# Other chunk sizes, a new order of the blocks, and one more block in paired products, in a two-layer trunk kernel

## The chip, the core and the metric

The kernel runs on one core of one Trainium2 chip. The metric is device time in microseconds, the median of three executions. Before the change these are 264.13, 264.52 and 264.88 us.

## What is computed

Two layers, each with three groups of attention heads side by side, on 256 tokens of width 1024, all in fp32. Cut to what matters here:

```python
h = rms_norm(x, norm_g[layer])
sb_q, sb_k, sb_v, sb_g, mb_q, mb_k, mb_v, mb_g, mem_q, mem_g = split(h @ w_in[layer])   # 8 x 384 and 2 x 256 columns
o_sb  = stick_breaking_attention(sb_q, sb_k, sb_v) * silu(sb_g)          # 6 heads of 64
o_mb  = softmax_attention(rotary(mb_q), rotary(mb_k), mb_v) * silu(mb_g) # 6 heads, causal
mk, mv = split(rms_norm(mem, mem_norm_g[layer]) @ w_mem_kv[layer])       # 256 memory tokens, 2 x 256 columns
o_mem = memory_attention(mem_q, mk, mv) * silu(mem_g)                    # 4 heads
x = x + concat(o_sb, o_mb, o_mem) @ w_out[layer]
```

With 256 tokens and blocks of 256 keys, the block-sparse attention `mb` has one block only and is plain causal attention. A last RMSNorm follows the second layer.

## The kernel before, in words

**Products.** Every projection is a "piece": `sb_qk` (768 columns, first of layer 0), the others with 384 or 256 columns, and `wo0` and `wo1` (512 columns each of `w_out`). Each has 8 blocks of 128 rows, k = 0 to 7. The product runs in fp32r. A weight w is split into hi (w rounded to fp32r) and lo (w - hi), the activations likewise, and three products are added: hi x hi, hi x lo, lo x hi. The split weights go to the buffer `hl`, HLC = 6144 weight columns wide (a column here is one column of one k block, 128 values). The activations' hi and lo halves stand side by side in `T`.

**Paired products.** A piece whose name stands in `DBL` (lines 85 and 86) takes two of its three products in one. `tr_k` (line 593, weights stationary, tokens moving) then issues, for each 128 columns and each k, one product of 512 columns (hi weights against the hi and lo activations) and one of 256 (lo weights against hi). A piece outside `DBL` takes three of 256. The two halves of the paired result are added when the bank is emptied. For a gate, `gate_evac` (line 940) does that with a copy on ACT and an addition on DVE, and in layer 0 a further multiplication by the row scale `rbx` on DVE. Without the pair it is one multiplication on DVE where `rbx` is there.

**Weights.** A piece is loaded in chunks of `NK` or `NKP` k blocks (lines 28 to 31). A chunk is one DMA from SP's queue into `raw`. ACT then rounds it into hi (`hi_task`, line 504; `DVE_HI` is added to DVE's price so that ACT gets all but two), and DVE subtracts (`lo_task`, line 513). TensorE may use a chunk when its hi and its lo are whole. `load_task` (line 522) lets at most `LOADS` chunks be under way: chunk j waits until chunk j - LOADS has landed.

**The order.** Every engine's instruction stream is written out by a planner, `Sched` (lines 117 to 237). Each part of the work is a task with a priority, a smaller number going first. The planner picks the step that can start earliest by its own estimates, and among those that start within a slack (`SLACK`, `SLACK_PE`) the one of smallest priority. On the chip the engines follow that order and wait for each other by semaphores. `PRI` and the constants `P_...` are priorities. `urgent` (line 529) gives the splitting of weights the priority -5 as long as it is at most `URG` chunks ahead of the chunk that TensorE is at, and 60 beyond that. The pieces' order in a layer is `ORDER`. A piece in `KMAJ` runs k outside and its parts inside, the others the parts outside. The `x` transposed slices and other inputs are loaded behind given chunks (`X_AT`, `X0_AT`, `X1_AT`, `CST_AT`). `xT` slice k is needed for k block k of `sb_qk`.

**Attention.** Scores (`pair_scores`, line 782) use 64 rows of the array, values (`pair_task`, line 901) 64 columns, both for a pair of heads. So TensorE changes its tile shape when it goes there and back; one such stay is called a visit here. `SCG` and `PVG` say which pairs are ready to run together as a group, `CROWD` and `HOLD` how many others, or how long, a lone pair waits for company. Between the two, softmax or stick-breaking runs on ACT and DVE, and the weights are transposed through DRAM (`trip`, line 1018; trips in `HALVES` come back in eight DMAs, the others in four). `DVE_W` shifts the choice of the engine that normalises softmax weights. A pair's values are multiplied with the silu of its gate (`ev`), split into `mxhi` and `mxlo`, and then the pieces `wo0` and `wo1` run, k = 0 to 3 of both first in layer 0. `silu_task` (line 965) takes the gates named together in `SILU`: it loads the silu table into ACT, runs, and loads the table of exp and ln back.

**Between the layers**, the last products of `wo1` give the residual, its row statistics and norm, and sixteen transposes on TensorE give the next layer's `T`. The first piece of layer 1 is a memory piece, which needs none of that.

Of the kernel before, what the change touches and what calls it, by code (L numbers as in the profile page):

```python
# [25 lines left out]
HLC = 6144  # L26
RAWC = 17664 - 2 * HLC
NK = {256: 3, 384: 2, 512: 2, 768: 1}
NKP = {("sb_k", 0): 4, ("sb_v", 0): 4, ("sb_v", 1): 4, ("sb_g", 1): 1, ("mb_q", 1): 3, ("mb_k", 1): 1, ("mb_v",
       1): 3, ("mb_g", 0): 4, ("mb_g", 1): 4, ("mem_q", 0): 1, ("mem_q", 1): 4, ("mem_g", 0): 2, ("mem_g",  # L30
       1): 2, ("mk", 0): 4, ("mv", 1): 2, ("wo0", 0): 1, ("wo0", 1): 1, ("wo1", 0): 1, ("wo1", 1): 1}
KSPLIT = (4, 4)
KMAJ = (("sb_q", 1), ("sb_g", 0), ("mb_q", 1), ("mb_k", 0), ("mb_k", 1), ("mb_v", 0), ("mb_g", 1), ("mem_g",
        0), ("mem_g", 1), ("mk", 1), ("mv", 0), ("mv", 1))
NTRIP = (0, 0)
KORD = ((0, 1, 2, 3, 4, 5, 6, 7), (6, 7, 4, 5, 2, 3, 0, 1))
LAT_SAME, LAT_CROSS = 130.0, 240.0
# [1 line left out]
NORM_LATE = 1029.7  # L39
DG_LATE = 885.3  # L40
COLD = 3900.0
PRI = ({"sb": (-1630, -1778), "mb": (-1356, -1226), "mem": (-2596, -720)}, {"sb": (-1368, -1432), "mb": (-1664,
       -2820), "mem": (388, 534)})
P_EV = -1323
P_H0 = 1640
P_RX = -1156
P_M0 = -1936
P_RM = 417
P_M1 = 86
URG = 4  # L50
X_AT = {4: 4, 7: 5, 8: 6, 9: 7}
CST_AT = 18
X0_AT = 9
X1_AT = 10
DMA_GBS = {"w1": 340.0, "w15": 350.0, "w3": 410.0, "dump": 250.0, "ret": 257.0}
RING = 8
SP_ISSUE = 450.0
# [4 lines left out]
TRIP_LAT = 500.0  # L62
ML_W = 0.0
ML_T = 200.0
ML_S = 800.0
SPLIT = (30,)
LOADS = 9
P_LD = -31914
MEM_AT = 0
ORDER = (["sb_qk", "mb_k", "mb_q", "mv", "mem_q", "sb_v", "mb_v", "mk", "sb_g", "mb_g", "mem_g"], ["mk",  # L70
         "mb_k", "mb_q", "mv", "mem_q", "mem_g", "sb_k", "sb_q", "sb_v", "mb_v", "mb_g", "sb_g"])
NCH = {"sb": 3, "mb": 3, "mem": 2}
SILU = ((("sb", "mb"), ("mem",)), (("sb",), ("mb", "mem")))
TABLE = 1290.0
P_SILU = -372
SCG = (((("sb", 2), ("sb", 1)), (("sb", 0), ("mb", 1), ("mb", 0)), (("mb", 2),), (("mem", 1),), (("mem", 0),)),
       ((("sb", 1), ("sb", 2), ("mb", 0)), (("mem", 0), ("mb", 1)), (("mem", 1), ("mb", 2)), (("sb", 0),)))
PVG = (((("mem", 0), ("mb", 2)), (("sb", 2), ("mb", 1), ("mb", 0)), (("sb", 1),), (("mem", 1),), (("sb", 0),)),
       ((("mb", 1), ("sb", 0), ("mb", 2), ("mem", 1)), (("sb", 2), ("sb", 1)), (("mem", 0),), (("mb", 0),)))
HOLD = 15360.0  # L80
HALVES = [("F", 1, "sb", 2), ("F", 1, "mb", 0)]
CROWD = 190
SPARE1 = 2
SPARE2 = 2
DBL = (("sb_qk", 0), ("sb_q", 1), ("sb_k", 1), ("sb_g", 1), ("mb_g", 0), ("mb_g", 1), ("mem_q", 0), ("mem_q",
       1), ("mem_g", 0), ("mem_g", 1), ("mk", 0), ("mk", 1), ("mv", 1))
DVE_W = -295.9
AHEAD = 106
DVE_HI = 42039.2
SLACK_PE = 170.0  # L90
SLACK = 20.0


def _free(ap):
# [145 lines left out]
def hybrid_trunk(ctx: ExitStack, tc: tile.TileContext, x, mem, norm_g, w_in, w_mem_kv, w_out,  # L240
# [150 lines left out]
    class Piece:  # L391
        def __init__(self, name, layer, src, width):
            self.name, self.layer, self.width, self.src = name, layer, width, src
            self.nk = NKP.get((name, layer), NK[width])
            self.kord = KORD[layer] if name[:2] == "wo" else tuple(range(KT))
# [238 lines left out]
    def piece_steps(p, n):  # L634

        if (p.name, p.layer) in KMAJ:
            return [(k, c) for k in range(KT) for c in range(n)]
# [511 lines left out]
    def main():  # L1149
# [25 lines left out]
        for l in range(DEPTH):  # L1175
# [15 lines left out]
            def T_piece(n, X, nchunk, need, post):  # L1191
                p = pieces[n, l]
                accs = {}
                for k, c in piece_steps(p, nchunk):
# [6 lines left out]
                    if k == KT - 1:  # L1201
                        S.spawn(post(c, accs[c]), P_EV, S.cur.t)

# [20 lines left out]
            for h in range(SBH):  # L1224
                S.spawn(scan_head(l, h), PRI[l]["sb"][1] + h)
            for h in range(MEMH):
                S.spawn(soft_head(l, h, "mem"), PRI[l]["mem"][1] + h)
            for h in range(SBH):
# [159 lines left out]
```

## Time and profile before

| | |
|---|---|
| median of three executions | 264.52 us |
| the profiled execution | 263.76 us |
| its span, first to last instruction | 262.0 us |
| TensorE busy | 255.6 us, 98%, 1573 products |
| its weight loads | 226.2 us, 86% |
| DVE busy | 223.5 us, 85%, 530 instructions |
| ACT busy | 193.8 us, 74%, 420 instructions |
| moved by DMA | 67.05 MB, 256 GB/s over the span |
| granted TensorE clock | 0.996 of full speed |

The profile lists each engine's busy time, the groups of instructions by line with their mean duration, the waits with who ended them, and the chain of work that ended last. A product's time from the start of one to the start of the next is shorter than its listed duration, since products overlap. So the text works with stretches of the trace that hold a counted number of products. PE is TensorE, PEld its weight loads, and `L299` line 299 of the kernel, where all DVE operations on two tensors are issued, whatever they work on; the names of the tiles tell them apart.

### The profile page before, as it was taken

How to read it: one execution, taken by the hardware profiler on the slowest of the kernel's cores; microseconds unless marked ns; L12 is line 12 of the kernel's file. 1: busy time of each engine (PE TensorE's matmuls, PEld its weight loads, DVE VectorE, ACT ScalarE, POOL GpSimd, SP SyncE). 2: the span in 40 equal slices, each digit the busy share in tenths (PEclk: the TensorE clock that was granted, in tenths of full speed). 3: DMA queues.
4: the chain of work that ended last, by engine and by line, in shares of the span. 5: the costliest groups of instructions: out<-in, count | busy, mean ns of one | idle time of the engine just before them, and what ended most of it. 6: DMA issues, size and time to landing. Idle time of an engine off the chain costs nothing.

```text
span 262.0 us, 4829 instructions
## 1 busy us (share of the span) xinstructions
PE 255.6 (98%) x1573; PEld 226.2 (86%) x1573; DVE 223.5 (85%) x530; ACT 193.8 (74%) x420; POOL 6.4 (2%) x18
## 2 busy tenths in 40 slices
PE   8999999999999999999999999999999999999991
PEld 5889999899899787878889998888899998788881
DVE  3876999999799999999899876779999999967454
ACT  3879996998797499994866654576958999786034
POOL 1001110001000000000000000000000000000000
PEclk9999999999999999999999999999999999999998
DMA  6999989999898999988665789784588888961004
GB/s 209 381 403 395 389 263 338 298 296 333 267 287 270 282 330 301 308 260 282 170 224 177 262 301 319 211 252 169 150 283 307 299 277 253 285 197 51 0 0 160
DMA packets 50200, 67.05 MB, mean 256 GB/s; under 512 B 4544, under 2 KB 41792, under 8 KB 50176
## 3 DMA queue, kind: packets, MB, share of 16 engines
q1 hardware_dynamic: 49232, 64.85, 77.4%
q0 software_dynamic: 512, 1.31, 1.7%
q10 hardware_dynamic: 432, 0.59, 0.7%
q8 instruction: 12, 0.20, 0.3%
q14 instruction: 12, 0.10, 0.1%
HBM read 57.29 MB, written 9.44 MB: 255 GB/s over the span
## 4 chain that ended last, share of the span: by engine, by line
PE 95%; ACT 1%; DMA 1%; DVE 0%; issue 0%; SPq 0%; DVEq 0%; ACTq 0%
PE bank L276 94%; DMA uT<-xT_dram 1%; PE bank L282 1%; ACT junk L295 1%; ACT ss L295 0%; DVE xs L299 0%; ACT T L295 0%; SPq L381 0%; DVE xs L307 0%; ACT xs L295 0%; DVEq L1384 0%; ACTq L295 0%
## 5 line engine op out<-in xcount | busy, mean ns | idle before, releaser
L299 DVE TENSOR_TENSOR hl<-raw,hl 128x512 fp32r<-128x512 f32 (+6 forms) x126 | 101.9, 825 | 7.8 <-ACT hl L293 5.7
L276 PE MATMUL bank<-T,hl 128*128 128x512 f32 (+1 forms) x606 | 104.5, 332 | 0.3 <-ACT T L295 0.3
L276 PEld LDWEIGHTS bank<-T,hl 128*128 128x128 f32 x606 | 90.2, 189 | 13.2 <-issue 1.2
L293 ACT CAST hl<-raw 128x512 fp32r<-128x512 f32 (+6 forms) x124 | 88.6, 740 | 16.9 <-PE bank L276 6.7
L276 PE MATMUL bank<-hl,T 128*128 128x384 f32 (+2 forms) x464 | 79.5, 330 | 0.0
L276 PEld LDWEIGHTS bank<-hl,T 128*128 128x128 f32 x464 | 77.5, 188 | 1.4 <-issue 0.7
L276 PE MATMUL bank<-hl,mxhi 128*128 128x512 f32 (+1 forms) x144 | 41.3, 367 | 0.0
L276 PEld LDWEIGHTS bank<-hl,mxhi 128*128 128x128 f32 x144 | 26.1, 189 | 5.0 <-ACT T L295 0.4
L276 PE MATMUL bank<-hl,mxlo 128*128 128x512 f32 (+1 forms) x72 | 26.4, 367 | 0.0
L295 ACT ACTIVATE junk<-xs 128x512 bf16<-128x512 f32 (+1 forms) x12 | 7.3, 611 | 17.6 <-DVE xs L299 16.2
L894 DVE STREAM_TRANSPOSE D<-w 128x384 f32<-128x384 f32 (+1 forms) x32 | 18.9, 594 | 0.4 <-ACT w L295 0.2
L295 ACT ACTIVATE w<-w,st 128x256 f32<-128x256 f32 (+1 forms) x32 | 14.1, 457 | 5.2 <-DVE st L847 4.5
L276 PEld LDWEIGHTS bank<-hl,mxlo 128*128 128x128 f32 x72 | 13.6, 188 | 2.2
L827 DVE TENSOR_TENSOR_SCAN a<-a,a 128x256 f32<-128x256 f32 (+1 forms) x24 | 12.7, 534 | 0.1
L295 ACT ACTIVATE T<-uT,gc 128x256 fp32r<-128x256 f32 x24 | 10.9, 508 | 2.0 <-DMA uT<-xT_dram 2.0
L303 DVE SCALAR_TENSOR_TENSOR T<-uT,gc,T 128x256 fp32r<-128x256 f32 x24 | 11.2, 480 | 0.9 <-ACT T L295 0.9
L295 ACT ACTIVATE a<-a 128x384 f32<-128x384 f32 x24 | 11.6, 522 | 0.2
L295 ACT ACTIVATE a<-bank 128x384 f32<-128x384 f32 x24 | 11.3, 483 | 0.0
L293 ACT COPY gT<-bank 128x256 f32<-128x256 f32 x13 | 4.8, 373 | 8.4 <-PE bank L276 8.2
L299 DVE TENSOR_TENSOR xs<-bank,xs 128x512 f32<-128x512 f32 (+1 forms) x8 | 5.2, 655 | 6.6 <-PE bank L276 6.6
L307 DVE TENSOR_SCALAR w<-w,st 128x256 f32<-128x256 f32 (+1 forms) x32 | 9.0, 324 | 0.1
L299 DVE TENSOR_TENSOR ev<-bank,gT 128x256 f32<-128x256 f32 x16 | 6.3, 417 | 1.5 <-ACT gT L295 1.4
(107 smaller groups left out, 217.9 us busy)
## 6 DMA issues: line engine op xcount, KB each, us to landing
raw<-in_w_in_dram SPq DMA_DIRECT2D x34, 384.0 KB, 6.0
raw<-in_w_out_dram SPq DMA_DIRECT2D x32, 256.0 KB, 5.0
Z<-D SPq DMA_DIRECT2D x16, 384.0 KB, 5.3
raw<-in_w_in_dram SPq DMA_DIRECT2D x7, 768.0 KB, 7.0
raw<-in_w_in_dram SPq DMA_DIRECT2D x18, 192.0 KB, 4.6
raw<-in_w_in_dram SPq DMA_DIRECT2D x4, 576.0 KB, 4.4
uT<-memT_dram SPq DMA_DIRECT2D x8, 256.0 KB, 6.8
raw<-in_w_in_dram SPq DMA_DIRECT2D x8, 256.0 KB, 5.5
```

The costliest lines, as they stand in the source:

```text
L276: nc.tensor.matmul(out, lhsT=lhsT, rhs=rhs, start=start, stop=stop, **kw)
L282: nc.tensor.transpose(out, in_, idt)
L293: nc.scalar.copy(out, in_)
L295: nc.scalar.activation(out, in_, func, **kw)
L299: nc.vector.tensor_tensor(out, a, b, op=op)
L303: nc.vector.scalar_tensor_tensor(out, a, s, b, op0=op0, op1=op1)
L307: nc.vector.tensor_scalar(out, a, s, None, op0=op)
L827: nc.vector.tensor_tensor_scan(a[:, r0:r1], a[:, r0:r1], u[:, r0:r1], 0.0, OP.add, OP.add)
L894: nc.vector.transpose(o, w[:, :n * 128].rearrange("p (m j r) -> p m j r", j=4, r=32))
```

## The change

Only constants change; no function does. With the chunk sizes given, the chunks are 138 in place of 126: 67 in place of 63 in layer 0, and 71 in place of 63 in layer 1. `("sb_g", 0)` joins `DBL`. The silu groups of layer 0 are three in place of two, the value groups there four in place of five. Ten loads may be under way in place of nine. `URG` goes from 4 to 63, and the slacks and all priorities get other values.

```diff
--- before.py
+++ after.py
@@ -26,12 +26,12 @@
 HLC = 6144
 RAWC = 17664 - 2 * HLC
 NK = {256: 3, 384: 2, 512: 2, 768: 1}
-NKP = {("sb_k", 0): 4, ("sb_v", 0): 4, ("sb_v", 1): 4, ("sb_g", 1): 1, ("mb_q", 1): 3, ("mb_k", 1): 1, ("mb_v",
-       1): 3, ("mb_g", 0): 4, ("mb_g", 1): 4, ("mem_q", 0): 1, ("mem_q", 1): 4, ("mem_g", 0): 2, ("mem_g",
-       1): 2, ("mk", 0): 4, ("mv", 1): 2, ("wo0", 0): 1, ("wo0", 1): 1, ("wo1", 0): 1, ("wo1", 1): 1}
+NKP = {("sb_k", 0): 4, ("sb_k", 1): 1, ("sb_v", 0): 1, ("sb_v", 1): 1, ("sb_g", 0): 4, ("mb_q", 0): 1, ("mb_q",
+       1): 1, ("mb_k", 1): 4, ("mb_v", 0): 1, ("mb_v", 1): 4, ("mb_g", 0): 3, ("mem_q", 0): 1, ("mem_g", 1): 1,
+       ("mk", 1): 1, ("mv", 0): 4, ("mv", 1): 2, ("wo0", 0): 3, ("wo0", 1): 3, ("wo1", 0): 3}
 KSPLIT = (4, 4)
-KMAJ = (("sb_q", 1), ("sb_g", 0), ("mb_q", 1), ("mb_k", 0), ("mb_k", 1), ("mb_v", 0), ("mb_g", 1), ("mem_g",
-        0), ("mem_g", 1), ("mk", 1), ("mv", 0), ("mv", 1))
+KMAJ = (("sb_q", 1), ("sb_v", 1), ("sb_g", 1), ("mb_q", 1), ("mb_v", 0), ("mb_g", 1), ("mem_q", 1), ("mem_g",
+        0), ("mem_g", 1), ("mv", 0))
 NTRIP = (0, 0)
 KORD = ((0, 1, 2, 3, 4, 5, 6, 7), (6, 7, 4, 5, 2, 3, 0, 1))
 LAT_SAME, LAT_CROSS = 130.0, 240.0
@@ -39,19 +39,19 @@
 NORM_LATE = 1029.7
 DG_LATE = 885.3
 COLD = 3900.0
-PRI = ({"sb": (-1630, -1778), "mb": (-1356, -1226), "mem": (-2596, -720)}, {"sb": (-1368, -1432), "mb": (-1664,
-       -2820), "mem": (388, 534)})
-P_EV = -1323
-P_H0 = 1640
-P_RX = -1156
-P_M0 = -1936
-P_RM = 417
-P_M1 = 86
-URG = 4
-X_AT = {4: 4, 7: 5, 8: 6, 9: 7}
-CST_AT = 18
+PRI = ({"sb": (-1812, -2078), "mb": (-1828, -1422), "mem": (-2720, -1120)}, {"sb": (-1568, -1708),
+       "mb": (-1916, -3416), "mem": (-810, 1014)})
+P_EV = -1461
+P_H0 = 1010
+P_RX = -1030
+P_M0 = -1630
+P_RM = 359
+P_M1 = -270
+URG = 63
+X_AT = {4: 4, 5: 5, 6: 6, 11: 7}
+CST_AT = 24
 X0_AT = 9
-X1_AT = 10
+X1_AT = 11
 DMA_GBS = {"w1": 340.0, "w15": 350.0, "w3": 410.0, "dump": 250.0, "ret": 257.0}
 RING = 8
 SP_ISSUE = 450.0
@@ -62,33 +62,33 @@
 TRIP_LAT = 500.0
 ML_W = 0.0
 ML_T = 200.0
-ML_S = 800.0
+ML_S = 300.0
 SPLIT = (30,)
-LOADS = 9
-P_LD = -31914
+LOADS = 10
+P_LD = -24288
 MEM_AT = 0
-ORDER = (["sb_qk", "mb_k", "mb_q", "mv", "mem_q", "sb_v", "mb_v", "mk", "sb_g", "mb_g", "mem_g"], ["mk",
-         "mb_k", "mb_q", "mv", "mem_q", "mem_g", "sb_k", "sb_q", "sb_v", "mb_v", "mb_g", "sb_g"])
+ORDER = (["sb_qk", "mb_q", "mb_k", "sb_v", "mem_q", "mk", "mv", "mb_g", "mb_v", "sb_g", "mem_g"], ["mv",
+         "mb_q", "mb_k", "mk", "mb_g", "mem_q", "sb_k", "sb_q", "mb_v", "sb_v", "mem_g", "sb_g"])
 NCH = {"sb": 3, "mb": 3, "mem": 2}
-SILU = ((("sb", "mb"), ("mem",)), (("sb",), ("mb", "mem")))
+SILU = ((("sb",), ("mb",), ("mem",)), (("sb",), ("mb", "mem")))
 TABLE = 1290.0
-P_SILU = -372
-SCG = (((("sb", 2), ("sb", 1)), (("sb", 0), ("mb", 1), ("mb", 0)), (("mb", 2),), (("mem", 1),), (("mem", 0),)),
-       ((("sb", 1), ("sb", 2), ("mb", 0)), (("mem", 0), ("mb", 1)), (("mem", 1), ("mb", 2)), (("sb", 0),)))
-PVG = (((("mem", 0), ("mb", 2)), (("sb", 2), ("mb", 1), ("mb", 0)), (("sb", 1),), (("mem", 1),), (("sb", 0),)),
-       ((("mb", 1), ("sb", 0), ("mb", 2), ("mem", 1)), (("sb", 2), ("sb", 1)), (("mem", 0),), (("mb", 0),)))
-HOLD = 15360.0
-HALVES = [("F", 1, "sb", 2), ("F", 1, "mb", 0)]
-CROWD = 190
+P_SILU = 934
+SCG = (((("sb", 2), ("sb", 0)), (("sb", 1), ("mb", 0), ("mb", 1)), (("mem", 1),), (("mem", 0),), (("mb", 2),)),
+       ((("mb", 0), ("sb", 0)), (("mb", 1), ("mem", 0), ("mb", 2)), (("sb", 1), ("sb", 2)), (("mem", 1),)))
+PVG = (((("mb", 0), ("sb", 2), ("sb", 1), ("mb", 1)), (("mem", 0), ("mb", 2)), (("mem", 1),), (("sb", 0),)),
+       ((("mem", 1), ("sb", 0), ("mb", 1), ("mem", 0)), (("mb", 2), ("sb", 1)), (("mb", 0),), (("sb", 2),)))
+HOLD = 12000.0
+HALVES = [("F", 1, "mb", 2)]
+CROWD = 104
 SPARE1 = 2
 SPARE2 = 2
-DBL = (("sb_qk", 0), ("sb_q", 1), ("sb_k", 1), ("sb_g", 1), ("mb_g", 0), ("mb_g", 1), ("mem_q", 0), ("mem_q",
-       1), ("mem_g", 0), ("mem_g", 1), ("mk", 0), ("mk", 1), ("mv", 1))
-DVE_W = -295.9
-AHEAD = 106
-DVE_HI = 42039.2
-SLACK_PE = 170.0
-SLACK = 20.0
+DBL = (("sb_qk", 0), ("sb_q", 1), ("sb_k", 1), ("sb_g", 0), ("sb_g", 1), ("mb_g", 0), ("mb_g", 1), ("mem_q",
+       0), ("mem_q", 1), ("mem_g", 0), ("mem_g", 1), ("mk", 0), ("mk", 1), ("mv", 1))
+DVE_W = 504.1
+AHEAD = 51
+DVE_HI = 63339.2
+SLACK_PE = 10.0
+SLACK = 0.0
 
 
 def _free(ap):
```

## The prediction

> **What bounds the kernel now.** First the page's busy times and its chain that ended last, then the waits of TensorE, then the chain in order of time.
>
> ```profile
> PE 255.6 (98%) x1573; PEld 226.2 (86%) x1573; DVE 223.5 (85%) x530; ACT 193.8 (74%) x420; POOL 6.4 (2%) x18
> ```
>
> ```profile
> PE 95%; ACT 1%; DMA 1%; DVE 0%; issue 0%; SPq 0%; DVEq 0%; ACTq 0%
> ```
>
> ```profile
> PE bank L276 <- PEq L1372: 0.8, 1, 0.8
> PE bank L276 <- ACT T L295: 0.3, 1, 0.3
> ```
>
> ```profile
> 4.59 128.15 PE bank L276 x796
> ...
> 139.26 114.49 PE bank L276 x696
> ...
> 258.25 0.33 DVEq L1384
> ```
>
> TensorE starts its real work at 4.59 us and is on the chain from there until 139.26 + 114.49 = 253.75 us, with only the sixteen transposes between the two long rows, which are TensorE's too. Its two waits, 1.1 us in all, lie in the first microseconds. So what the change can win lies in the 4.59 us before, in the last 262.0 - 253.75 = 8.25 us, in the number of products, and in what it costs to change tile shape. What it can lose is anything that comes later than TensorE wants it. DVE at 85% and ACT at 74% are not bounds over the whole span, but both are nearly full in stretches, so their order matters.
>
> A busy TensorE may still be slow inside, so I take counted stretches: the piece `sb_g` of layer 0 (72 products of 256 columns), a run of paired products in layer 1 (36 of 512 and 36 of 256; the count in the row holds a neighbour or two at the edges), and two visits for values, of 8 and of 24 products.
>
> ```profile
> 76.94:85.58 8.64, 8.64 (x74) 1.00 0.88 267
> 159.74:172.51 12.77, 12.77 (x73) 1.00 0.88 272
> 87.43:88.23 0.80, 0.80 (x10) 1.00 1.00 357
> 240.68:242.78 2.10, 2.10 (x25) 1.00 0.00 0
> ```
>
> Three products of 256 cost 8.64 / 24 = 0.360 us, a pair of 512 and 256 costs 12.77 / 36 = 0.355 us. A visit of 8 value products takes 0.80 us and one of 24 takes 2.10 us, so 16 more take 1.30, 8 take 0.65, and 0.15 us goes to the change of shape inside the visit. The last product before a visit is slowed too, which the next row shows: four products of 256 columns start at 42.77 and the visit at 43.34, 0.57 us in place of 4 x 0.12.
>
> ```profile
> 42.77 0.64 PE L276 MATMUL bank<-hl,T 128*128 128x256 f32 x4
> 43.34 1.58 PE L276 MATMUL bank<-sb_k,sb_q 64*128 64x128 f32 x16
> ```
>
> That is 0.09 us more. A visit costs 0.15 to 0.3 us beyond its products; the upper end grants the return the same as the way there.
>
> **The change part by part.**
>
> *The pair for `sb_g`.* It has 3 x 8 = 24 pairs in place of 24 triples: 24 x 0.005 = 0.12 us less on TensorE, on the path. It costs other engines the emptying of the banks:
>
> ```profile
> L299 DVE TENSOR_TENSOR gT<-bank,gT 128x256 f32<-128x256 f32 x13 | 5.3, 415 | 2.6 <-ACT gT L293 2.6
> L299 DVE TENSOR_TENSOR gT<-gT,rbx 128x256 f32<-128x256 f32 x5 | 2.1, 410 | 0.0
> L299 DVE TENSOR_TENSOR gT<-bank,rbx 128x256 f32<-128x256 f32 x3 | 1.1, 393 | 0.0
> L293 ACT COPY gT<-bank 128x256 f32<-128x256 f32 x13 | 4.8, 373 | 8.4 <-PE bank L276 8.2
> ```
>
> DVE pays 3 x (0.415 + 0.410 - 0.393) = 1.3 us more and ACT 3 x 0.373 = 1.1 us more. Both lie beside products.
>
> *Chunk sizes.* The columns stay, the number of chunks goes from 126 to 138. What one more chunk costs comes from two sizes:
>
> ```profile
> L299 DVE TENSOR_TENSOR hl<-raw,hl 128x512 fp32r<-128x512 f32 x46 | 30.6, 682 | 2.5 <-DMA F<-Z 1.2 <-ACT hl L293 0.8 <-PE bank L276 0.5
> L299 DVE TENSOR_TENSOR hl<-raw,hl 128x1536 fp32r<-128x1536 f32 x8 | 13.8, 1738 | 0.0
> L293 ACT CAST hl<-raw 128x512 fp32r<-128x512 f32 x46 | 26.9, 619 | 4.9 <-PE bank L276 3.3 <-DMA raw<-in_w_in_dram 1.4 <-DMA raw<-in_w_out_dram 0.2
> L293 ACT CAST hl<-raw 128x1536 fp32r<-128x1536 f32 x8 | 11.9, 1482 | 2.5 <-DMA raw<-in_w_in_dram 2.1 <-PE bank L276 0.4
> ```
>
> Three chunks of 512 cost DVE 2.05 us, one of 1536 costs 1.74, so a chunk's fixed part is 0.15 us; on ACT (1.857 - 1.482) / 2 = 0.19 us. Twelve more chunks cost DVE 1.8 us and ACT 2.3 us over the whole span, hidden. What is not hidden by itself is the size at a place where TensorE is close behind: a chunk of 1536 can be used only when it is whole, 1.48 + 1.74 = 3.2 us after ACT takes it, against 1.3 us for one of 512. The pieces `wo0` and `wo1` of layer 0 now come in chunks of three k blocks and one. That is the first rival.
>
> *Normalising softmax weights.* `DVE_W` rises by 800 ns, so some of this leaves DVE:
>
> ```profile
> L307 DVE TENSOR_SCALAR w<-w,st 128x256 f32<-128x256 f32 x22 | 7.1, 348 | 0.0
> L307 DVE TENSOR_SCALAR w<-w,st 128x128 f32<-128x128 f32 x10 | 2.7, 273 | 0.1
> ```
>
> It is at most 7.1 + 2.7 = 9.8 us, over both layers. Summed, DVE has 223.5 + 1.3 + 1.8 and 0 to 9.8 us less, 217 to 227 us, and ACT more: neither comes to TensorE's 255.6. Zero on the path, with TensorE's products as cover.
>
> *One silu group more.* It adds two table loads in layer 0.
>
> ```profile
> 99.48 1.28 ACT L971 ACT_TABLE_LOAD   x1
> 100.77 1.48 ACT L295 ACTIVATE gT<-gT 128x1536 f32<-128x1536 f32 x1
> 102.28 1.28 ACT L973 ACT_TABLE_LOAD   x1
> 103.57 1.66 ACT L293 CAST hl<-raw 128x512 fp32r<-128x512 f32 x3
> ```
>
> That is 2 x 1.28 = 2.6 us of ACT, and the next operation starts 1.29 us after the load's start. Behind each load are queued the hi casts of the next chunks. Where this ends on the path is the second rival. The Trainium skill, "ScalarE: Activation LUTs", section "What ACT_TABLE_LOAD costs", gives 2.66 us for a switch, load and drain together, so by that page the added group would take ACT 5.3 us; its section "Table sets: the hidden batching unit" asks to batch calls by set, which speaks against this edit. The rows show the load without a drain behind it, and they decide.
>
> *First loads.* `xT` slices 5 and 6 now come earlier, so the chunk for k = 4 lands behind one slice more, and slice 7 comes behind 0.5 MB of `x` and two chunks of 192 KB.
>
> ```profile
> 4.59:13.44 8.85, 8.85 (x54) 1.00 0.99 358
> 13.44:19.80 6.36, 6.36 (x38) 1.00 1.05 403
> ```
>
> ```profile
> 10.76 2.83 DVE L299 TENSOR_TENSOR hl<-raw,hl 128x768 fp32r<-128x768 f32 x3
> ...
> 16.09 0.48 DVE L303 SCALAR_TENSOR_TENSOR T<-uT,gc,T 128x256 fp32r<-128x256 f32 x1
> ```
>
> The first 54 products are k = 0 to 3, and 36 more are k = 4 to 6, so TensorE begins k = 4 at 13.44 and k = 7 at 19.80 us. The chunk for k = 4 is the second of the three splits and is ready near 12.65 us; 128 KB at about 400 GB/s, the rate in the second row, is 0.33 us, leaving 0.46. Slice 7 is ready at 16.57; 0.92 MB are 2.3 us, so 18.9 against 19.80. Both hold: zero, at worst some tenths if ACT and DVE are taken by something else just then.
>
> *Order, groups, priorities, ten loads, one trip in halves fewer.* No product comes or goes with them. Five value groups of layer 0 were run in three visits, since lone pairs join others; four groups can be two to four. I take no change, and one visit each way as bounds, 0.3 us. Ten loads in place of nine put more on SP's queue ahead of the trips, and the smaller chunks take as much off; four DMAs fewer of 48 KB on SP. Zero, where weights are ahead. The last stretch, from the last product to the output, keeps its operations.
>
> The sum against the profiled execution: 263.76 - 0.12 = 263.6 us. The median lies 0.76 us above that execution, so I forecast 264.52 - 0.12 = 264.4 us: no difference, since about 0.3% (0.8 us) is what a measurement of this kernel can tell from none.
>
> **The rivals.**
>
> *`wo1` of layer 0 waits for its first chunk (slower, 0.14).* TensorE starts `wo0` at 105.51 and, after 24 products of 512 columns at 0.355 - 0.12 = 0.235 us, `wo1` at about 111.1.
>
> ```profile
> 105.51 0.40 PE L276 MATMUL bank<-hl,mxhi 128*128 128x512 f32 x1
> ```
>
> ```profile
> 108.69 0.68 DVE L299 TENSOR_TENSOR hl<-raw,hl 128x512 fp32r<-128x512 f32 x1
> ...
> 110.63 0.68 DVE L299 TENSOR_TENSOR hl<-raw,hl 128x512 fp32r<-128x512 f32 x1
> ```
>
> These are the first and the third chunk of `wo1`, ready at 109.37 and 111.31. As one chunk, all three are there at 111.31 at the earliest, 0.2 us late, and if DVE can begin only after one cast of 1536, 1.7 us late: 264.6 to 266.1 us, say 265.5. It decides from 0.8 us of wait. Against it: `URG` of 63 always puts splitting ahead of tasks with a priority above -5, so weights should be further ahead than before.
>
> *The silu for `sb` comes late (slower, 0.06).* `sb_g` is now the last gate but one, and `wo0` begins with the products of `sb`. In the profile, after the silu:
>
> ```profile
> 103.35 0.75 DVE L299 TENSOR_TENSOR ev<-bank,gT 128x256 f32<-128x256 f32 x2
> 104.02 0.48 DVE L314 CAST mxhi<-ev 128x256 fp32r<-128x256 f32 x2
> 104.42 0.75 DVE L299 TENSOR_TENSOR mxlo<-ev,mxhi 128x256 fp32r<-128x256 f32 x2
> ```
>
> They end at 105.17, `wo0` starts at 105.51: 0.34 us of room. If the `mb` group's table loads fall just before, 2.6 us less that room are 2.2 us: 266.6 us. The weaker priority of silu (934, behind -5 for casts) speaks for it, the shorter silu (768 elements a row in place of 1536) against. By the 2.66 us a switch of the Trainium skill ("ScalarE: Activation LUTs", the section named above) it would be 5.0 us and 269.4 us; the rows bear out none of the difference.
>
> *The norm between the layers is late (slower, 0.05).*
>
> ```profile
> 135.69 0.69 DVE L299 TENSOR_TENSOR T<-bank,T 128x512 fp32r<-128x512 f32 x1 [0.50 <-ACT T L293]
> ...
> 140.22 0.69 DVE L299 TENSOR_TENSOR T<-bank,T 128x512 fp32r<-128x512 f32 x1
> ```
>
> ```profile
> 136.99 1.83 PE L276 MATMUL bank<-hl,T 128*128 128x384 f32 x9
> ```
>
> `T` is ready at 136.38, and TensorE uses it at 136.99: 0.6 us of room. The cover, a memory piece of 256 columns, keeps its length. With `URG` 63 splits go ahead of the norm's steps; two of 1536 in the way are 3.5 us less 0.6, 267.3 us.
>
> *Fewer visits (faster, 0.15).* Three visits fewer are 0.9 us, 263.5 us. Against it: lone pairs already join others.
>
> **How the numbers follow.** No difference has 0.60: the sum is 0.12 us and TensorE has no stall to give back. The three slower cases have 0.25 together, since the room at all three places is under 1 us while every order changes; the faster one has 0.15. The range goes from 263.3 (the visits and the pair, and a tenth or two at the start) to 266.1 us (the late chunk at its worst); left out are the late silu, the late norm and a little below. The likeliest case's own range is 263.9 to 264.9 us.
>
> **What would show it.** TensorE still at 98% with no wait beyond the start; 24 products of 512 more and 48 of 256 fewer; a stretch of `sb_g` of 8.5 us; ten table loads beside the first; nine visits. Wrong would be a wait of TensorE's on `hl` or `mxhi` near 105 to 112 us, on `T` near 137 us, or seven visits or fewer.

## The result

| | before | after |
|---|---|---|
| median, same chip | 264.16 us (6 executions, 263.94 to 264.88) | 267.14 us (6 executions, 267.05 to 268.51) |
| the profiled execution | 263.76 us | 268.40 us |
| its span | 262.0 us | 266.6 us |

The ratio is 1.0124, 95% interval 1.0097 to 1.0151: the changed kernel is slower by 3.0 us by the medians and 3.3 us by the ratio, and the measured time lies above the forecast range. Here and below, ratios leave out the executions that took over 1.5% longer than the fastest of the same kernel (one of 281.79 and one of 271.86 us), while medians and ranges hold all.

### The profile page after: what moved, and what is told of

Its sections match the earlier page's. It is cut to its first block, busy times and chain, and to the rows that moved or that the text cites. A ratio compares the mean times of both kernels' runs of the same rounds, so it can differ in the third digit from the quotient of the medians.

```text
span 266.6 us, 4840 instructions
## 1 busy us (share of the span) xinstructions
PE 258.0 (97%) x1549; PEld 225.6 (85%) x1549; DVE 223.4 (84%) x530; ACT 202.2 (76%) x453; POOL 6.2 (2%) x18
## 4 chain that ended last, share of the span: by engine, by line
PE 88%; DMA 4%; ACT 4%; DVE 2%; issue 1%; SPq 0%; DVEq 0%; ACTq 0%
PE bank L276 87%; DMA raw<-in_w_out_dram 3%; DMA uT<-xT_dram 1%; DVE st L860 1%; PE bank L282 1%; ACT junk L295 1%; ACT L973 0%; ACT L971 0%; ACT hl L293 0%; ACT ss L295 0%; ACT T L295 0%; DVE hl L299 0%; ACT gT L295 0%; DVE xs L299 0%; ACT gT L293 0%
## 5 line engine op out<-in xcount | busy, mean ns | idle before, releaser
L299 DVE TENSOR_TENSOR hl<-raw,hl 128x384 fp32r<-128x384 f32 (+5 forms) x138 | 103.7, 765 | 9.8 <-ACT hl L293 9.6
L276 PE MATMUL bank<-T,hl 128*128 128x512 f32 (+1 forms) x582 | 103.4, 338 | 0.7 <-ACT T L295 0.7
L276 PEld LDWEIGHTS bank<-T,hl 128*128 128x128 f32 x582 | 88.8, 188 | 14.4 <-issue 1.2
L293 ACT CAST hl<-raw 128x384 fp32r<-128x384 f32 (+6 forms) x136 | 89.7, 695 | 14.1 <-PE bank L276 9.1
L276 PE MATMUL bank<-hl,T 128*128 128x384 f32 (+2 forms) x464 | 80.7, 331 | 0.0
L276 PE MATMUL bank<-hl,mxhi 128*128 128x512 f32 (+1 forms) x144 | 43.0, 378 | 1.8 <-ACT mxhi L293 1.5
L276 PE MATMUL bank<-hl,mxlo 128*128 128x512 f32 (+1 forms) x72 | 27.3, 379 | 0.0
L295 ACT ACTIVATE w<-w,st 128x256 f32<-128x256 f32 (+1 forms) x50 | 21.3, 463 | 2.8 <-DVE st L847 2.6
L293 ACT COPY gT<-bank 128x256 f32<-128x256 f32 x16 | 5.8, 374 | 5.4 <-PE bank L276 5.3
L847 DVE CUSTOM_DVE_ANT_0 w<-bank,cmask 128x128 f32<-128x128 f32 (+1 forms) x24 | 7.2, 353 | 1.7 <-PE bank L276 1.6
```

The source lines that it names most:

```text
L276: nc.tensor.matmul(out, lhsT=lhsT, rhs=rhs, start=start, stop=stop, **kw)
L293: nc.scalar.copy(out, in_)
L295: nc.scalar.activation(out, in_, func, **kw)
L299: nc.vector.tensor_tensor(out, a, b, op=op)
L847: nc.vector.tensor_tensor_reduce(w[:, r0:r1], sc[:, r0:r1], cmask[:, 256 - r1 + r0:256], -1.0, 3.0e38, OP.add, OP.min, st[:, t:t + 1])
```

## The profile after

The page of the changed kernel: busy times, the granted clock in 40 slices, and the shares of the chain that ended last.

```profile
PE 258.0 (97%) x1549; PEld 225.6 (85%) x1549; DVE 223.4 (84%) x530; ACT 202.2 (76%) x453; POOL 6.2 (2%) x18
...
PEclk9999999999999999799999999999999999999999
...
PE 88%; DMA 4%; ACT 4%; DVE 2%; issue 1%; SPq 0%; DVEq 0%; ACTq 0%
```

TensorE has 24 products fewer, as the pair asks, and is yet busy 2.4 us longer. The chain is no longer TensorE's alone: ACT and DMA hold 8% of it. One slice, 106.6 to 113.3 us, has a lower clock. The waits of TensorE (engine and line, what it waited for: us in total, times, longest):

```profile
PE bank L276 <- ACT mxhi L293: 1.5, 1, 1.5
PE bank L276 <- PEq L1372: 0.8, 1, 0.8
PE bank L276 <- ACT T L295: 0.7, 1, 0.7
PE bank L276 <- DVE mxhi L314: 0.2, 1, 0.2
```

Two are new, for `mxhi`, and both lie where `wo0` of layer 0 begins. TensorE's order of time there, with the idle time before each group in brackets:

```profile
102.79 1.52 PE L276 MATMUL bank<-T,mb_v 128*64 128x256 f32 x16
104.14 1.47 PE L276 MATMUL bank<-F,sb_v 128*64 128x256 f32 x16
107.13 0.49 PE L276 MATMUL bank<-hl,mxhi 128*128 128x512 f32 x1 [1.52 <-ACT mxhi L293]
...
108.56 0.50 PE L276 MATMUL bank<-hl,mxhi 128*128 128x512 f32 x1 [0.23 <-DVE mxhi L314]
...
109.58 1.06 PE L276 MATMUL bank<-hl,mxhi 128*128 128x512 f32 x2
110.43 0.63 PE L276 MATMUL bank<-hl,mxlo 128*128 128x512 f32 x1
```

Without the first wait `wo0` would have begun at 107.13 - 1.52 = 105.61 us, 0.10 us later than before (105.51), with the same products behind it but for the pair. So nearly all of the loss lies behind this point.

The last two rows show a second loss. Two products of 512 columns take 110.43 - 109.58 = 0.85 us, 0.43 us each, where one took about 0.235 us before.

For the reason of the first wait one reads ACT's order of time, where `mxhi` of the first block is rounded:

```profile
96.42 1.48 ACT L293 CAST hl<-raw 128x1536 fp32r<-128x1536 f32 x1
...
98.86 0.61 ACT L293 CAST hl<-raw 128x512 fp32r<-128x512 f32 x1
100.26 2.00 ACT L293 CAST hl<-raw 128x1536 fp32r<-128x1536 f32 x2 [0.78 <-DMA raw<-in_w_out_dram]
102.28 1.28 ACT L971 ACT_TABLE_LOAD   x1
103.57 0.84 ACT L295 ACTIVATE gT<-gT 128x768 f32<-128x768 f32 x1
...
106.67 0.40 ACT L293 CAST mxhi<-ev 128x256 fp32r<-128x256 f32 x1
```

The first two casts are `wo0`'s four blocks, three and one. The next row is `wo1`'s four blocks. Before the change three of `wo1`'s first four casts came behind the silu, and all four subtractions behind the value steps on DVE. Now all stand ahead, and the first of the casts waits 0.78 us for a transfer of 768 KB. The silu's input was whole at 101.54 us (the row below), but the silu runs at 103.57. On DVE, in order of time:

```profile
101.16 0.38 DVE L299 TENSOR_TENSOR gT<-gT,rbx 128x256 f32<-128x256 f32 x1
101.46 2.95 DVE L299 TENSOR_TENSOR hl<-raw,hl 128x512 fp32r<-128x512 f32 x3
104.45 1.08 DVE L299 TENSOR_TENSOR ev<-bank,gT 128x256 f32<-128x256 f32 x3
...
107.55 0.75 DVE L299 TENSOR_TENSOR ev<-bank,gT 128x256 f32<-128x256 f32 x2
```

Behind the silu DVE takes one `sb` pair and both `mb` pairs first, and the two `sb` pairs that `wo0` needs next only at 107.55. The three subtractions in the second row are of `wo0`'s fourth block and of `wo1`. Layer 1 and the end of the kernel show no wait. From the trace, the changed kernel has eleven visits where the old one had nine.

## The experiments

Each kernel was timed beside the kernel before on the same chip. Unless said otherwise the base is the kernel after, and the planner's own prices are left as they were, so that the order of all that is not named stays. The code shown is cut to the lines that matter.

**The kernel after again, as the base.**

> The changed kernel once more, as it is, to have it beside the edits. Both theories: 267.1 us where the granted clock is 0.998, and 268.4 us in an execution where it is 0.993, since in the profile the products after the wait near 107 us take 0.427 us in place of 0.229 for about 4 us.

267.43 us (266.19 to 269.42), ratio 1.0117, interval 1.0081 to 1.0152. Its executions scatter over 3.2 us. TensorE's order of time, and its row for 105 to 113 us (us, busy us of each engine, then the granted clock), first of this run:

```profile
107.16 0.49 PE L276 MATMUL bank<-hl,mxhi 128*128 128x512 f32 x1 [1.26 <-ACT mxhi L293]
```

```profile
105.00:113.00 8.00, 6.48 (x35) 4.38 (x32) 7.63 (x21) 7.96 (x15) 0.00 (x0) 1.00 0.98 355
```

and the same stretch of the changed kernel's first profile:

```profile
105.00:113.00 8.00, 6.22 (x22) 4.09 (x19) 7.49 (x20) 7.96 (x15) 0.00 (x0) 0.79 0.96 355
```

The waits are there again, the lower clock is not. So the waits belong to the kernel, and the slow products to some of its executions. The six executions of the result above agree: four have a mean granted clock of 0.998 or 0.999 and took 267.05 to 267.15 us, the two with 0.993 and 0.991 took 268.40 and 268.51 us.

**The pair undone, the order kept.** `sb_g` of layer 0 has three products of 256 again.

```diff
+        if (p.name, p.layer) == ("sb_g", 0):
+            nc.tensor.matmul(acc[:, 0:256], lhsT=hi[:, o:o + 128], rhs=X[0][:, k, :], start=first, stop=False)
+            nc.tensor.matmul(acc[:, 0:256], lhsT=hi[:, o:o + 128], rhs=X[1][:, k, :], start=False, stop=False)
+            nc.tensor.matmul(acc[:, 0:256], lhsT=lo[:, o:o + 128], rhs=X[0][:, k, :], start=False, stop=last)
...
```

> The changed kernel with sb_g of layer 0 in three products of 256 columns as before, its banks emptied by one multiplication on DVE at the place of the former addition, everything else in the order of the changed kernel. Theory A: the gates are ready 0.9 us sooner and nothing comes of it, since ACT's table load waits for the casts before it; with 24 x 0.005 us more on TensorE 267.2 us. Theory B: the wait falls by 0.9 us, 266.3 us. Theory C: 267.2 us.

267.12 us, ratio 1.0104 (1.0086 to 1.0123), and the wait for `mxhi` is 1.5 us as before. The pair is not the cause.

**The rounding of sb0's value on DVE in place of ACT.**

```diff
-        copy(mxhi[:, k, :], m, e)
...
+            nc.vector.tensor_copy(mxhi[:, k, :], m)
...
```

> The changed kernel with every order kept but one: the hi half of the first value block (k = 0 of sb in layer 0) is made on DVE in place of ACT, where it stands behind the table load back, two gate copies and a scaling, and its lo half right behind it. Theory A (the chain silu, values, mxhi sets the wait): 1.0 to 1.4 us less, about 265.9 us, and a first wait of TensorE's under 0.4 us. Theories B and C: no difference, 267.1 us.

267.06 us, 1.0116 (1.0083 to 1.0148). The waits of TensorE in this run:

```profile
PE bank L276 <- DVE mxhi L314: 1.2, 1, 1.2
PE bank L276 <- DVE mxhi L936: 0.8, 1, 0.8
```

The first block's wait falls from 1.3 to 0.8 us (L936 is the moved step), and the second block's grows from 0.2 to 1.2. The wait has moved on by one block.

**wo1's first conversions behind the silu, twice.** Chunks 61 and 62 are `wo1`'s first four blocks.

```diff
-            copy(his(j), raws(j), e)
+            if j in (61, 62):
+                held["hi"].append(j)
...
+            else:
+                copy(his(j), raws(j), e)
...
+        if (l, kind, c) == (0, "sb", 0):
+            for j in held["hi"]:
+                nc.scalar.copy(his(j), raws(j))
```

The subtractions are held in the same way.

> The changed kernel with every order kept but one: the two casts of wo1's first weights in layer 0 (1536 and 512 columns) come after the first mxhi on ACT, their subtractions after the first mxlo on DVE. Theory A (the first output product waits because the silu of sb stands behind these casts on ACT): TensorE's wait of 1.5 us before the first mxhi product falls below 0.3 us and the time by 1.7 to 2.2 us, 265.0 to 265.4 us. Theory B (the paired sb_g empties its banks in three steps, so the gates are late): no difference, 267.1 us. Theory C (the output weights themselves are late, in chunks of 1536): slower by up to 0.5 us, since they come later still.

277.59 us, 1.0502 (1.0471 to 1.0532). This edit did not do what it was made for: its casts and subtractions come behind a load into the same `raw` block, so they work on other weights. ACT waits 7.0 us for these, and TensorE waits 9.9 us for the value steps behind them. It tells nothing of the cause. The second try holds the loads back as well.

> The changed kernel with one change of order: the casts of wo1's first weights in layer 0 (1536 and 512 columns) come after the first mxhi on ACT, their subtractions behind the value steps of sb on DVE, and the loads that follow on those buffers behind these. Theory A1 (the silu of sb is late because it stands behind these casts): silu about 2 us sooner, the products of k = 1 start 1.2 us sooner, 1.0 to 1.3 us less than the changed kernel beside it (267.4 us there), 266.2 us. Theory A2 (what follows the silu on DVE is in the wrong order: the steps of mb stand before those of sb that TensorE needs first): under 0.4 us less. Theory C (the output weights are late): slower.

267.40 us, 1.0105 (1.0079 to 1.0131). The wait at `wo0`'s start is nearly gone (of the two waits for `mxlo` below, the one of 0.2 us lies there and the other at 125.8 us), but the time is not:

```profile
PE bank L276 <- DMA T<-Z: 1.2, 1, 1.2
PE bank L276 <- DVE mxlo L299: 0.8, 2, 0.6
```

`T` is here the softmax weights of a memory pair, on their way back from the transposition through DRAM. They are late now. The held loads stand on SP's queue ahead of others, which waited 2.4 us there for the moved subtraction.

**The steps of sb ahead of those of mb on DVE**, with sb0's rounding there too.

```diff
+        back = l == 0 and kind == "mb" and c < 2
+        first = (l, kind, c) == (0, "sb", 0)
...
+        if back:
+            behind.append(values)
...
+        if (l, kind, c) == (0, "sb", 2):
+            for f in behind:
+                f()
```

> The changed kernel with one change of order: after the silu of sb in layer 0, DVE takes the value steps of the three sb pairs first (k = 0, 1, 2, hi of k = 0 on DVE too) and those of two mb pairs (k = 3, 4) behind them. Theory A2: TensorE's wait for k = 0 and k = 1 falls from 2.2 to 0.3 to 0.9 us, the time by about 1.4 us, 266.0 us. Theory A1: under 0.4 us less. Theory C: no difference.

266.94 us (266.12 to 269.26), 1.0111 (1.0071 to 1.0152). In its profile, taken in the fastest of its executions, the waits for `mxhi` are gone, and one of 0.6 us for the memory pair (`T<-Z`) has come.

**Both of these edits together.**

> Both changes of order at once: casts of wo1's first weights behind the silu of sb, and the value steps of sb ahead of those of mb. If the 2.2 us of waits at the start of the output product are what the changed kernel loses there, the waits fall below 0.4 us and the time by 1.8 to 2.2 us, 265.2 to 265.6 us; what then stays above the kernel before (264.2 us) is 1.0 to 1.4 us, of which the two more visits of TensorE to the attention shapes are 0.6. If the output weights are what is late behind it (theory C), less than 1 us is gained.

270.04 us, 1.0224 (1.019 to 1.0257): the wait for `T<-Z` is 2.5 us. In this profile the granted clock is also 0.62 from 120 to 124 us and 0.53 from 124 to 128 us, so not all of the time need be the held loads' own. Nothing is won by the two orders together.

**The silu for sb left out**, with its table loads (the gates are copied).

```diff
+        if l == 0 and kinds == ("sb",):
+            act(g, g, AF.Copy)
...
```

> The changed kernel without the table loads of the added silu group: the gates of sb in layer 0 are copied in place of going through silu, so that part of the computation is left out. The order stays. If one silu group more is what costs: the gates are 1.3 us sooner and mxhi of k = 0 2.6 us sooner, 1.3 to 1.6 us less than the changed kernel, about 265.9 us. Theory A2: the value steps of mb still stand before those of sb, which are not done before 107 us, so at most 0.5 us less.

267.14 us, 1.0103 (1.0077 to 1.0129). No wait for ACT is left at `wo0`, but 0.9 us for `mxlo` and 0.4 us for `T<-Z`. Up to here the first theory, one late silu, has fallen: whoever is taken away, somebody else is late by about as much. SP's queue shows why the memory pair is. First the kernel before, then the kernel after:

```profile
104.44 0.84 SPq L381 DMA_DIRECT2D raw<-in_w_out_dram  x2
105.33 6.43 SPq L1035 DMA_DIRECT2D T<-Z  x8
```

```profile
103.84 1.02 SPq L381 DMA_DIRECT2D raw<-in_w_out_dram  x2
104.95 1.54 SPq L381 DMA_DIRECT2D raw<-in_w_mem_kv_dram  x2
106.55 8.86 SPq L1035 DMA_DIRECT2D T<-Z  x8
```

The eight DMAs of the two returns are all issued by 111.76 us before, and by 115.41 after. The returns' issues (L1035) wait on SP for loads of `wo` to land, from 92 to 119 us, before and after:

```profile
SPq L1035 <- DMA raw<-in_w_out_dram: 2.5, 4, 1.3
```

```profile
SPq L1035 <- DMA raw<-in_w_out_dram: 4.7, 6, 1.6
```

The returns also take longer, and so does the way out (`Z<-D`). The DMA issues from 85 to 125 us, with KB each and the median us from issue to landing, before and after:

```profile
raw<-in_w_out_dram SPq DMA_DIRECT2D x13, 256.0 KB, 5.2
...
Z<-D SPq DMA_DIRECT2D x2, 512.0 KB, 5.2
T<-Z SPq DMA_DIRECT2D x8, 128.0 KB, 5.4
```

```profile
raw<-in_w_out_dram SPq DMA_DIRECT2D x4, 768.0 KB, 7.3
...
Z<-D SPq DMA_DIRECT2D x2, 512.0 KB, 6.7
T<-Z SPq DMA_DIRECT2D x8, 128.0 KB, 6.5
```

Out and back are 10.6 us before and 13.2 us after. The loads beside them now come in 768 KB. That these make the trip longer is likely from the rows, but no run tests it alone.

**The memory pairs' return on GpSimd's queue**, with the `sb` order of above and alone.

```diff
-                nc.sync.dma_start(Fv[32 * j:32 * j + 32, i0:i1],
+                q = nc.gpsimd if name[:3] == ("F", 0, "mem") else nc.sync
+                q.dma_start(Fv[32 * j:32 * j + 32, i0:i1],
```

> The steps of sb1 and sb2 stand before those of mb0 and mb1 on VectorE and sb0's rounded value is made there (as in the run before that did only this), and the transposed weights of layer 0's two mem pairs come back from DRAM on GpSimd's queue and not on SP's. Theory 'one wait hides the next': both late values are then in time, the waits of TensorE between 105 and 122 us are under 0.4 us in sum, and what is left over the kernel before is two visits more at 0.3 us and the start, so 264.8 to 265.4 us. Rival 'the difference lies elsewhere': the median stays at 266.9 although the waits are gone. Rival 'the trip is no quicker on the other queue': the wait for T before the visit at about 116 us is there again, 0.6 us or more, 266.7 to 267.5.

> The kernel after with the mem pairs' return alone on GpSimd's queue; the order of the value steps as in the kernel after. Theory 'one wait hides the next': the wait of 1.3 to 1.5 us for sb0's rounded value is there as before and the mem pair's return was behind it already, so 266.6 to 267.4, no different from the kernel after. Rival 'the return of the mem weights is the bound by itself': 265.6 or less.

With both: 266.09 us (265.72 to 266.74), 1.0068 (1.0047 to 1.009). Alone: 267.54 us, 1.0133 (1.0104 to 1.0163); its profile, at 269.37 us, has a wait for `mxhi` of 2.1 us and a granted clock of 0.57 from 108 to 112 us. So one wait did hide the next, and both edits together give back about 1.2 us where neither alone gives anything that shows. But 2.0 us are left, 0.7 more than the theory had. In the profile of the first, which took 266.74 us, the spacing of its products shows about 2 us still lost in small waits between 105 and 125 us.

**Work in the wait.** Seven products on constants ahead of `wo0`'s first.

> The kernel after with seven products of 512 columns of a constant in bfloat16 ahead of the first product of wo0 in layer 0; they fill the wait of 1.5 us and their result is overwritten. Theory 'the clock falls after the wait': TensorE has work through it, no execution is above 267.5 and the median comes to 266.2 to 266.8, the profile shows no products at 0.427 us. Rival 'the scatter is the transfers': executions from 266.2 to above 268 as before, median 266.9 to 267.5.

267.36 us (266.87 to 268.44), 1.0123 (1.01 to 1.0145). The profile has no product at 0.43 us from `wo0` on, and the median is where it was. TensorE still waits 0.8 us behind the filling, since the value came later in this execution. The lower clock is not what the median pays.

**What a visit costs**, on the kernel before.

```diff
+                    if l == 1 and n in ("sb_v", "mb_v") and 0 < k < KT - 1:
+                        j, o = p.loc(k, 0)
+                        nc.tensor.matmul(accs[t][:, 384:512], lhsT=X[0][0:64, k, t * 128:(t + 1) * 128],
+                                         rhs=his(j)[0:64, o:o + 128], start=False, stop=False, skip_group_check=True)
```

> The kernel before with 24 visits more: inside the values' pieces sb_v and mb_v of layer 1, after each block but the last and the first one, one product of 64 rows by 128 columns stands between those of 128 rows, in columns of the bank that nobody reads. If a visit costs 0.3 us as the prediction took it, whatever its length, 24 x 0.3 = 7.2 us, so 271.4. Rival: a visit of one product costs its entry and exit of 0.1 us each alone and the product is hidden, 24 x 0.2 = 4.8, 269.0. Rival: nearly nothing but the product's own 0.05 to 0.11 us, 265.5 to 266.8.

274.44 us, 1.0389 (1.0368 to 1.041): (274.44 - 264.05) / 24 = 0.43 us for one (one of the 24 stands beside a stay that was there anyway). In TensorE's order of time:

```profile
203.55 0.79 PE L276 MATMUL bank<-hl,T 128*128 128x384 f32 x3
204.27 0.32 PE L1214 MATMUL bank<-hl,T 64*128 64x128 f32 x1
204.52 0.79 PE L276 MATMUL bank<-hl,T 128*128 128x384 f32 x3
```

The visit takes 204.52 - 204.27 = 0.25 us, and the three products ahead of it take 204.27 - 203.55 = 0.72 us. They take 0.52 us where nothing is between them, 0.173 us from start to start. So 0.2 us of a visit is paid by its neighbours. About 0.35 us is left for a visit when its one product's own share is taken off, an estimate at 0.65 / 8 = 0.08 us a product, the prediction's row for visits.

**Three things undone**: the two of the combined run and the silu for `sb`.

> As the run with sb's steps first and the mem pairs' return on GpSimd's queue, and the gates of sb in layer 0 are copied in place of the silu, without the two table loads (so another function is computed for them, and 2.6 us of ScalarE are gone just ahead of wo0). Theory 'the same late chain in smaller waits': the 1.1 us of waits from 105.9 to 110 us go, what is left over the kernel before is two visits at 0.3 to 0.4 us, some 0.3 at the start of the kernel and at most 0.6 for the last mem pair, so 264.8 to 265.5 us. Rival 'something other than waits': 265.9 to 266.3 as without it.

266.95 us (266.12 to 267.36), 1.0095 (1.0074 to 1.0115): no gain over the combined run; the median is higher, though the two intervals meet. TensorE's order of time, with its longest wait here, and GpSimd's queue:

```profile
120.27 1.08 PE L276 MATMUL bank<-T,mv 128*64 128x256 f32 x8 [1.07 <-DVE hl L299]
```

```profile
111.58 2.17 POOL L1064 DMA_DIRECT2D T<-Z  x4 [4.64 <-DMA Z<-D]
```

This is the visit of the last memory pair. The bracket names a subtraction on DVE, but TensorE's queue has ahead of the visit an instruction that waits for the four DMAs of the pair's return. The last of them, issued at 113.20, lands at 120.13 us by its semaphore events, and that ends the wait. So it is the memory pair again, on a queue of its own: GpSimd waits 4.6 us for the way out (`Z<-D`), issues from 111.58 on, and the last DMA takes 6.9 us to land. So SP's queue was only part of it; the way out and the landing stay long on the other queue too.

**How much room the silu had**, on the kernel before: the gates are copied onto themselves once, or twice, ahead of it.

```diff
+        if l == 0 and "sb" in kinds:
+            for _ in range(1):
+                nc.scalar.copy(g, g)
```

> The kernel before with one copy of the gates onto themselves, 1536 columns on ScalarE, ahead of its first silu in layer 0: the silu and all behind it on ScalarE start about 1.4 us later. Theory 'wo0 waits for the silu, with 0.34 us of room as the prediction reckoned': 1.4 - 0.34 = 1.1 us more, 265.2, with a wait of TensorE for mxhi or ev before wo0. Rival 'there is more room': 264.0 to 264.5. Rival 'a late silu costs more than itself, for the casts behind it are late too': 265.8 or more.

> The same with two copies, about 2.8 us. Theory: 2.8 - 0.34 = 2.5 us more than the kernel before, 266.6. Rival 'more room': 265.6 or less. Rival 'more than itself': 267.5 or more.

One copy: 264.23 us, 0.9999 (0.9985 to 1.0014). Two: 265.89 us, 1.0061 (1.0045 to 1.0078). A copy takes 1.5 us, so 1.5 us cost nothing and 3.0 us cost 1.7. The first value step on DVE in the kernel before, then with one copy, then with two:

```profile
102.18 1.25 DVE L299 TENSOR_TENSOR hl<-raw,hl 128x512 fp32r<-128x512 f32 x2
103.35 0.75 DVE L299 TENSOR_TENSOR ev<-bank,gT 128x256 f32<-128x256 f32 x2
```

```profile
103.96 0.76 DVE L299 TENSOR_TENSOR ev<-bank,gT 128x256 f32<-128x256 f32 x2 [0.48 <-ACT gT L295]
```

```profile
106.35 0.76 DVE L299 TENSOR_TENSOR ev<-bank,gT 128x256 f32<-128x256 f32 x2 [1.99 <-ACT gT L295]
```

In the kernel before, the step waits for DVE's conversions and not for the silu. That is part of the room.

**The chunks of wo in layer 0**, from three sides: `wo1`'s conversions left out of the kernel after; chunks of three blocks put into the kernel before; chunks of two put into the kernel after. In the last two the planner makes its own order.

```diff
-       1): 2, ("mk", 0): 4, ("mv", 1): 2, ("wo0", 0): 1, ("wo0", 1): 1, ("wo1", 0): 1, ("wo1", 1): 1}
+       1): 2, ("mk", 0): 4, ("mv", 1): 2, ("wo0", 0): 3, ("wo0", 1): 1, ("wo1", 0): 3, ("wo1", 1): 1}
```

> The kernel after without the conversions of wo1's four chunks in layer 0, the cast on ScalarE and the subtraction on VectorE; the products of wo1 in layer 0 read what stood in the buffers before, so its output is not the layer's. Order of all else as in the kernel after. Theory 'conversions of wo's three-block chunks stand ahead of the value steps': the waits at the start of wo0 go, no other takes their place above 0.4 us in sum, 264.8 to 265.4 us, which are the two visits and the start. Rival 'the value steps are late by themselves, with VectorE and ScalarE free': the waits for mxhi or for T stay, 266.2 to 267.2.

> The kernel before with the weights of wo in layer 0 in chunks of three blocks and one (three of 512 columns, then one), and nothing else of the change; the program puts its own order together again, with the same nine visits. Theory 'three-block chunks of wo': TensorE waits for the value steps at the start of wo0, 1.0 to 2.2 us, 265.2 to 266.6 us. Rival 'it needs the rest of the change (groups of values, a silu of its own for sb)': 263.9 to 264.6.

> The kernel after with those chunks of two blocks in place of three and one; the order is put together again. Theory: casts of 1.0 in place of 1.5 us and shorter transfers behind which the silu waits, so about a third of the waits goes, 266.2 to 266.8 us. Rival 'chunk size does not matter': 266.9 to 267.5.

Without the conversions: 266.64 us (265.93 to 268.81), 1.008 (1.0052 to 1.0109). The wait for ACT at `wo0` is gone, and the memory pair's return is late. The profile is of the slowest execution, 268.81 us, so its wait is larger than the median can hold; three of the six took 265.93 to 266.10 us.

```profile
PE bank L276 <- DMA T<-Z: 2.7, 2, 2.5
```

So the conversions alone are not it; the large loads stayed. The kernel before with chunks of three: 268.50 us (267.71 to 271.86), ratio 1.0147 (1.0121 to 1.0172). Two constants, with the order that the planner makes of them, bring the whole loss, and more. It has twelve visits and not nine, against what was expected of it, which at 0.35 us are 1.0 of the 3.9 us. In its profile, which took 267.80 us, waits of the same kind make 1.8 us: 1.3 for the memory pair's return and 0.5 at `wo0`'s start for a gate's copy on ACT. What is left is not assigned. DVE's order of time, then TensorE's longest wait:

```profile
100.80 4.59 DVE L299 TENSOR_TENSOR hl<-raw,hl 128x512 fp32r<-128x512 f32 x4
105.31 0.75 DVE L299 TENSOR_TENSOR ev<-bank,gT 128x256 f32<-128x256 f32 x2
```

```profile
PE bank L276 <- DMA T<-Z: 1.3, 1, 1.3
```

The silu was done at 103.47 us, but `ev` starts at 105.31, behind 4.6 us of conversions, all but the first of `wo`; 103.35 us was its time with chunks of one. The kernel after with chunks of two: 265.45 us (265.32 to 266.53), 1.0045 (1.0028 to 1.0062), the best of the variants of the kernel after. ACT's order of time there:

```profile
99.67 1.04 ACT L293 CAST hl<-raw 128x1024 fp32r<-128x1024 f32 x1
100.73 1.28 ACT L971 ACT_TABLE_LOAD   x1
102.02 0.84 ACT L295 ACTIVATE gT<-gT 128x768 f32<-128x768 f32 x1
...
105.12 1.04 ACT L293 CAST hl<-raw 128x1024 fp32r<-128x1024 f32 x1
```

The silu comes 1.55 us earlier than in the changed kernel, and `wo1`'s casts are behind it again. Its visits are the same eleven. No variant beats the kernel before.

## Why the prediction was wrong

**The failed step: "Chunk sizes", with the sentence "What is not hidden by itself is the size at a place where TensorE is close behind".** It found the right place, `wo0` and `wo1` of layer 0 in chunks of three, but asked only when TensorE could use the weights. TensorE never waited for `hl` there. What the size does is to make the conversions and the loads into long, indivisible items in queues that run in order: 1.48 us on ACT, 1.76 on DVE, 768 KB on SP. They stand ahead of the silu, the value steps and the memory pairs' return. The prediction even argued against its first rival that weights would be further ahead than before. That they were is what made the other steps late. Chunks of two in place of three take the ratio from 1.0124 to 1.0045, about 2.1 us of 3.3 us. The visits are eleven in both, but the order is made anew, so that number holds for size and order together.

**"Zero, where weights are ahead"**, for the order, groups and ten loads, failed for the same reason: a queue with weights ahead is a queue with something behind them. The return's eight DMAs are issued 3.65 us later on SP, and out and back take 2.6 us longer. The order also took away a cover. Before, the last eight products of `mem_g` stand between the values' visit and `wo0`'s first product, from 103.99 to 105.51 us. In the kernel after `wo0` comes right behind that visit, so 1.5 us less are left for the silu, the values and their rounding. No run tests this alone, and the kernel after with chunks of two has no such cover either and keeps a wait of 0.5 us for `mxhi`.

**"I take no change, and one visit each way as bounds, 0.3 us"** was off twice. The visits went from nine to eleven, and one costs about 0.35 us, at the top or a bit over the stated 0.15 to 0.3. Two would be 0.7 us, and with the 2.1 us of the chunks 2.8 of some 3.3 us. That is a sum and not a measurement. One of the two lies ahead of `wo0`, and up to there the trace has lost only 0.10 us, though TensorE also started 0.23 us later (4.82 against 4.59). So at least the one ahead of `wo0` does not show its price, and half a microsecond or more is not assigned.

**The pair, 0.12 us**, is too small to see: undoing it left 267.12 against 267.43 us.

**The room of 0.34 us at wo0** was read from the end of the second block's `mxlo` (105.17), while TensorE's first product needs the first block's `mxhi` alone, which starts at 104.02 and takes 0.28 us. So the room of that step was 1.2 us, and the late silu cost nothing up to 1.5 us. The second rival named the silu, and the first wait in the profile is its sign, `mxhi` with 1.5 us. Its reason was wrong: `mb`'s table loads run some 20 us earlier (the first at 80.85 us), and what stands ahead of the silu are casts of `wo1`.

**What held**: 24 products fewer in all, ten table loads beside the first, neither DVE nor ACT the bound over the whole span (223.4 and 202.2 us), the norm between the layers, which shows no wait, and the first loads to some tenths (the wait for `T` at the start is 0.7 us in the first profile and 0.3 in the second, where it was 0.3). The range was too narrow above since each rival was priced as one late thing. Here at least three were late within 15 us, each hidden by the one ahead of it.

**Open**: how the 2.1 us divide among the conversions, the loads and the order of the value steps. Leaving out the conversions of `wo1` gives 266.64 us, working round the late value and the late return 266.09, and the two were not combined with smaller chunks. The kernel after with chunks of one was not run, nor was `URG`, which puts the splitting of weights ahead, put back alone. Why the run with three things undone has a median 0.9 us above that with two is known from one profile each, where the return lands at 120.13 and 119.34 us.

## What to carry to other kernels

A larger conversion is cheaper by itself (here by 0.15 to 0.19 us for each chunk saved), but where a queue is worked off in order, its price is paid by whatever short, urgent step stands behind it: list what follows it on each queue it goes through, not only who uses its result. When removing a wait does not move the time, look for the next late thing a few microseconds on before giving up the theory, and undo the two together. To find the cause, put the suspected constant alone into the old kernel: that brought the loss in one run, after eleven edits of the new one had only moved it. Where a planner makes the order anew, count what else changed, here three visits.

## What the runs showed of the hardware

- After waits of 1.5 and 0.2 us within 3 us, products of 512 columns took 0.43 us each for some 4 us and the granted clock was 0.79 over 105 to 113 us. In another execution of the same kernel with waits of 1.3 and 0.2 us the clock stayed at 1.00, and so it did after a wait of 2.5 us in the run without conversions. After a wait of 2.1 us in the run with the return alone on GpSimd's queue it was 0.57 from 108 to 112 us, and around a wait of 2.5 us in the run with both orders 0.62 from 120 to 124 us and 0.53 from 124 to 128. In the run whose edit failed it was 0.50 from 112 to 120 us, in and after a wait of 9.9 us. What decides after the short waits is not known from these runs.
- A stay of a single product of 64 rows between products of 128 rows costs 0.43 us (24 of them on the kernel before), of which 0.2 us appears on the neighbouring products.
- A DMA of a return waits on SP's queue for earlier loads to land: from 92 to 119 us 2.5 us in all where the loads of `wo` are 256 KB, and 4.7 us where they are up to 768 KB.
